# A hybrid GLA/SSD layer: output gate, second norm and weight addresses rearranged

## The chip, the cores and the metric

The kernel is one program on one core of a Trainium2 chip. Its time is the device time in microseconds of one execution. Five engines work from queues of their own: TensorE (PE, with weight loads listed apart as PEld), VectorE (DVE), ScalarE (ACT), GpSimd (POOL) and SyncE (SP, which here issues most transfers). Each takes its instructions in the order in which the program put them there.

## What is computed

One layer over 512 latent tokens of width 1024, with 256 context tokens beside them. The part around the change, cut from the reference:

```python
ada = silu(c)[:, None, :] @ w_ada + b_ada
sh1, sc1, g1, sh2, sc2, g2 = jnp.split(ada, 6, axis=-1)
parts = _split_in(modulate(rms_norm(h_lat, norm1_w), sh1, sc1) @ w_in)   # q k v r ... z xs ... gates
# GLA branch (q, k, v, r) -> o_a @ w_pa = y_a;  SSD branch (z, xs, ...) -> o_b @ w_pb = y_b
merged = sigmoid(gate_a) * y_a + sigmoid(gate_b) * y_b
h_lat = h_lat + g1 * (merged @ w_out)
h2 = modulate(rms_norm(h_lat, norm2_w), sh2, sc2)        # h * (1 + scale) + shift
h_lat = h_lat + g2 * ((silu(h2 @ w_gate) * (h2 @ w_up)) @ w_down)
return rms_norm(h_lat, final_norm_w)
```

## The kernel before

Every large product is made of three matmuls (`mm3`): each operand is kept as a rounded high part and the low rest, and high x high, high x low and low x high add up in PSUM. Weights come as blocks of 512 KB, 128 partitions by 1024 floats. `load_raw` (L176) issues the load on SP into one of three raw buffers. `split_w` rounds the block to its high part on ACT (L188) and subtracts that on DVE (L189); `load_w` allots the two results, `whi` and `wlo`, from two buffers each. A block that doesn't find a free buffer waits there.

The program is one long row of stages: adaLN and the first norm; input projections by head (GLA) and by group (SSD), each followed by its scan; back projections `pa` and `pb` (`proj_back`, 512 columns of tokens streamed against weight columns); the merge gates; the last back projection, `pb` 3; the merge; the output projection; the second norm; the feed-forward. `proj_cols` keeps the weights stationary and streams tokens (`l_` for latent, `c_` for context). `proj_rows` (L386 to L388, for v, r and z) does the reverse: it keeps `hH` or `hL` stationary and streams 256 columns of weights. A scheduler with a model of durations sets the order within each engine's queue; weight splits have high priority in it.

In the tail, `merge(j)` is called as the columns of `pb` 3 are finished: two gate tiles are loaded, DVE adds one and multiplies by each branch (L977, L978), POOL adds the two branches (L979, `tgm`), ACT rounds the result to `mH` and DVE makes `mL` (L980, L981; the tiles are called `mt`, `mL`, `mLb`). Each `w_out` block is multiplied on POOL by the gate row `g1r` before its split (L187). The output projection (L204 to L206, `ob`) takes its first four weight blocks over all four token tiles, then blocks 4 to 7 (the last two in `w67`, shown as `w`) tile by tile, so that tile 0 finishes first.

Per tile of 128 tokens, DVE then adds `ob` to `hres` (L1012), ACT squares with a sum (L1014), DVE and POOL make the reciprocal root (`hs`, `rv_h`, `rr_h`), DVE multiplies the row by it and by the scale row (L1021, `hn`) and adds the shift row (L1022; one of eight on POOL), PE transposes (L1025, `hT`), ACT and DVE split the result into `h2H` and `h2L` (L1028, L1029). The scale and shift rows are loaded from a copy of the adaLN vector in DRAM and spread over 128 partitions. The low parts of the first two gate and up blocks are made on POOL (`split_pool`). These two blocks are multiplied in halves of 256 tokens (L1057 to L1059), the later ones, from j = 2, over 512.

Pad tiles at both ends of SBUF (`top_pad`, `low_pad`) are there so that the large tiles begin at multiples of 256 bytes; all weight, `hH` and `hL` operands of the three-matmul products do. `some_ada` computes later columns of the adaLN vector on POOL, a block at a time.

Of the kernel before, what the change touches and what calls it, by code (L numbers as in the profile page):

```python
# [129 lines left out]
def hybrid_layer_kernel(ctx: ExitStack, tc: tile.TileContext, x, xc, wts, vec, rows, up, msk, lvl, out):  # L130
# [808 lines left out]
    nc.sync.dma_start(g1r.rearrange("p (j c) -> p j c", c=P), arow[0:1, 16:24, :].to_broadcast([P, 8, P]))

    def half_rows(name, j0):
        ts = []
        for c in range(2):
            t = ch.tile([P, 512], F32, tag="s2", name=f"{name}_{c}", bufs=7)
            nc.sync.dma_start(t.rearrange("p (j c) -> p j c", c=P), arow[0:1, j0 + 4 * c:j0 + 4 * c + 4, :].to_broadcast([P, 4, P]))
            ts.append(t)
        return ts
# [257 lines left out]
```

## Time and profile before

| | |
|---|---|
| median of 3 runs | 1394.48 us (1393.54 to 1395.78) |
| the profiled execution, its own time | 1392.06 us |
| its span, first to last instruction | 1390.3 us |
| PE busy | 1339.7 us, 96% |
| DVE busy | 854.5 us, 61% |
| ACT busy | 523.5 us, 38% |
| POOL busy | 328.0 us, 24% |
| HBM | 121 GB/s over the span |

A busy PE is a PE with a matmul in flight: matmuls overlap, and the time from the start of one to the start of the next is shorter than the record of one. The shares are means over stages with different limits.

### The profile page before, as it was taken

How to read it: one execution, taken by the hardware profiler on the slowest of the kernel's cores; microseconds unless marked ns; L12 is line 12 of the kernel's file. 1: busy time of each engine (PE TensorE's matmuls, PEld its weight loads, DVE VectorE, ACT ScalarE, POOL GpSimd, SP SyncE). 2: the span in 40 equal slices, each digit the busy share in tenths (PEclk: the TensorE clock that was granted, in tenths of full speed). 3: DMA queues.
4: the chain of work that ended last, by engine and by line, in shares of the span. 5: the costliest groups of instructions: out<-in, count | busy, mean ns of one | idle time of the engine just before them, and what ended most of it. 6: DMA issues, size and time to landing. Idle time of an engine off the chain costs nothing.

```text
span 1390.3 us, 19141 instructions
## 1 busy us (share of the span) xinstructions
PE 1339.7 (96%) x7462; PEld 1140.9 (82%) x7462; DVE 854.5 (61%) x1317; ACT 523.5 (38%) x924; POOL 328.0 (24%) x277
## 2 busy tenths in 40 slices
PE   5998999999999999999999999999889999999997
PEld 3797999889889788878878887777688888888886
DVE  4659686572695687668769776668673433333235
ACT  6475343433445142633524352332333223222122
POOL 1356455244100211021021102116631312100001
PEclk9899999999999999999999999999999999999999
DMA  9453322423322333223323233557413333333331
GB/s 366 141 198 121 101 101 92 128 81 132 103 81 85 126 124 106 89 87 92 114 80 116 87 121 98 189 166 252 153 60 121 123 120 122 122 106 91 94 113 67
DMA packets 58010, 169.19 MB, mean 122 GB/s; under 512 B 6064, under 2 KB 10304, under 8 KB 57792
## 3 DMA queue, kind: packets, MB, share of 16 engines
q1 hardware_dynamic: 55328, 157.96, 34.6%
q0 software_dynamic: 2304, 9.64, 2.2%
q8 instruction: 59, 0.97, 0.3%
q10 hardware_dynamic: 288, 0.36, 0.1%
q14 instruction: 31, 0.25, 0.1%
HBM read 156.23 MB, written 11.72 MB: 121 GB/s over the span
## 4 chain that ended last, share of the span: by engine, by line
PE 82%; DVE 7%; DMA 6%; issue 2%; ACT 2%; POOL 2%; SPq 0%; POOLq 0%; DVEq 0%; ACTq 0%
PE up L1059 3%; PE gate L1058 3%; PE up L1058 3%; PE gate L1059 3%; PE gate L1057 3%; PE up L1057 3%; PE db L204 3%; PE db L205 3%; PE db L206 3%; DMA E<-cdr 2%; PE yi L501 2%; PE r_z L386 2%; PE r_z L388 2%; PE r_z L387 2%; PE l_xs L361 2%; PE pb_pb L633 2%
## 5 line engine op out<-in xcount | busy, mean ns | idle before, releaser
L341 POOL TENSOR_TENSOR raw_ada<-raw_ada,cs 128x1024 f32<-128x1024 f32 x32 | 66.9, 2090 | 279.0 <-DMA raw_ada<-in_wts_dram 233.1
L343 POOL TENSOR_TENSOR raw_ada<-raw_ada 128x512 f32<-128x512 f32 x64 | 77.6, 1213 | 4.3
L386 PE MATMUL r_z<-whi_z,hH 128*128 128x256 f32 x256 | 74.0, 289 | 0.9 <-DVE cv_x L663 0.9
L388 PE MATMUL r_z<-whi_z,hL 128*128 128x256 f32 x256 | 72.9, 285 | 0.0
L387 PE MATMUL r_z<-wlo_z,hH 128*128 128x256 f32 x256 | 72.8, 285 | 0.0
L1058 PE MATMUL gate<-h2L,whi_gate 128*128 128x512 f32 (+1 forms) x192 | 71.7, 373 | 0.0
L1057 PE MATMUL gate<-h2H,whi_gate 128*128 128x512 f32 (+1 forms) x192 | 71.7, 374 | 0.0
L1059 PE MATMUL gate<-h2H,wlo_gate 128*128 128x512 f32 (+1 forms) x192 | 71.4, 372 | 0.0
L753 ACT ACTIVATE E<-E,ebias 128x128 f32<-128x128 f32 x128 | 41.2, 391 | 65.1 <-DVE E L750 65.1
L1059 PE MATMUL up<-h2H,wlo_up 128*128 128x512 f32 x160 | 63.0, 394 | 0.0
L1058 PE MATMUL up<-h2L,whi_up 128*128 128x512 f32 x160 | 62.3, 389 | 0.0
L1057 PE MATMUL up<-h2H,whi_up 128*128 128x512 f32 x160 | 62.2, 389 | 0.0
L189 DVE TENSOR_TENSOR wlo_down<-raw_down,whi_down 128x1024 fp32r<-128x1024 f32 x18 | 22.0, 1225 | 62.4 <-ACT whi_down L188 62.3
L189 DVE TENSOR_TENSOR wlo_gate<-raw_gate,whi_gate 128x1024 fp32r<-128x1024 f32 x20 | 31.1, 1557 | 45.7 <-ACT whi_gate L188 45.7
L386 PE MATMUL r_v<-whi_v,hH 128*128 128x256 f32 x192 | 55.7, 290 | 0.4 <-ACT whi_v L188 0.4
L205 PE MATMUL db<-wlo_down,fH 128*128 128x512 f32 x142 | 55.2, 389 | 0.0
L206 PE MATMUL db<-whi_down,fL 128*128 128x512 f32 x142 | 55.2, 389 | 0.0
L388 PE MATMUL r_v<-whi_v,hL 128*128 128x256 f32 x192 | 55.1, 287 | 0.0
L387 PE MATMUL r_v<-wlo_v,hH 128*128 128x256 f32 x192 | 54.6, 284 | 0.0
L632 PE MATMUL pb_pb<-yT,whi_pb 128*128 128x512 f32 x128 | 54.2, 425 | 0.0
L1066 DVE TENSOR_TENSOR f<-f,up 128x512 f32<-128x512 f32 x22 | 15.1, 687 | 63.1 <-PE up L1059 62.5
L188 ACT ACTIVATE whi_gate<-raw_gate 128x1024 fp32r<-128x1024 f32 x22 | 23.3, 1060 | 76.7 <-PE gate L1058 67.2
...
## 6 DMA issues: line engine op xcount, KB each, us to landing
...
```

Source lines behind the costliest of these rows:

```text
L189: (nc.gpsimd if split_pool[0] else nc.vector).tensor_tensor(lo, raw, hi.bitcast(F32), ALU.subtract)
L205: nc.tensor.matmul(out_, aH, bL, start=False, stop=False)
L206: nc.tensor.matmul(out_, aL, bH, start=False, stop=stop)
L341: nc.gpsimd.tensor_tensor(raw, raw, cs[:, :, 0:1].to_broadcast([P, KD, P]), ALU.mult)
L343: nc.gpsimd.tensor_tensor(raw[:, 0:n, :], raw[:, 0:n, :], raw[:, n:2 * n, :], ALU.add)
L386: nc.tensor.matmul(o, hH[:, kk, tk], hi[:, k, :], start=st, stop=False, skip_group_check=True)
L387: nc.tensor.matmul(o, hH[:, kk, tk], lo[:, k, :], start=False, stop=False, skip_group_check=True)
L388: nc.tensor.matmul(o, hL[:, kk, tk], hi[:, k, :], start=False, stop=sp, skip_group_check=True)
L632: nc.tensor.matmul(pt, hi[:, k, cl], aH[:, k, :], start=(k == 0), stop=False)
L1057: nc.tensor.matmul(pts[kj][:, tk], hi[:, k, :], h2H[:, k, tk], start=(k == 0), stop=False)
L1058: nc.tensor.matmul(pts[kj][:, tk], hi[:, k, :], h2L[:, k, tk], start=False, stop=False)
L1059: nc.tensor.matmul(pts[kj][:, tk], lo[:, k, :], h2H[:, k, tk], start=False, stop=(k == KD - 1))
```

## The change

The gate g1 moves from the weights to the result: DVE multiplies each `ob` bank by `g1r` before it is added to `hres`. The merge's addition and the four low parts that POOL made are put on DVE.

The second norm is done by columns. ACT multiplies the rows by the reciprocal root alone (`hn`); PE transposes two token tiles into four banks, in which a channel is a partition; there scale and shift are one number per partition, and ACT (`h2H`) and DVE (`hv`, then `h2L`) apply them to 256 tokens at a time. The row copies of scale, shift and norm weight, with their six transfers, are gone, and only the 16 rows of g1 go through DRAM. The last eight columns of the adaLN vector start three feed-forward blocks later.

The `whi` and `wlo` buffers become 1088 floats long. Blocks of 256 columns (v, r, z, pa, pb) begin 48 floats, 192 bytes, into them; all others at their start, a multiple of 256 bytes.

```diff
-    def split_w(key, hi, lo, row=None):
+    def split_w(key, hi, lo):
         with nullcontext() if in_start[0] else tc.high_priority():
             raw = load_raw(key)
-            if row is not None:
-                nc.gpsimd.tensor_tensor(raw[:, 0, :], raw[:, 0, :], row, ALU.mult)
             nc.scalar.activation(hi, raw, AF.Copy)
-            (nc.gpsimd if split_pool[0] else nc.vector).tensor_tensor(lo, raw, hi.bitcast(F32), ALU.subtract)
+            nc.vector.tensor_tensor(lo, raw, hi.bitcast(F32), ALU.subtract)
...
-        hi = wp.tile([P, nk, ncol], F32R, tag="whi", name="whi_" + nm)
-        lo = wp.tile([P, nk, ncol], F32R, tag="wlo", name="wlo_" + nm)
+        c0 = 48 if ncol == 256 else 0
+        hi, lo = (wp.tile([P, 1088], F32R, tag="w" + p, name=f"w{p}_{nm}")[:, c0:c0 + nk * ncol].rearrange("p (k c) -> p k c", k=nk)
+                  for p in ("hi", "lo"))
...
-    nc.tensor.transpose(pt[0:96, 0:P], ada.rearrange("p j t -> p (j t)"), ident)
+    nc.tensor.transpose(pt[0:16, 0:P], ada[:, 16:24, :].rearrange("p j t -> p (j t)"), ident)
...
-    sh2 = half_rows("sh2", 24)
-    sc2 = half_rows("sc2", 32)
...
-        nc.vector.scalar_tensor_tensor(sc2[c], sc2[c], 1.0, n2, ALU.add, ALU.mult)
+    s2c = cst.tile([P, 64], F32, name="s2c")[:, 0:KD]
+    nc.vector.scalar_tensor_tensor(s2c, ada[:, 32:40, 0], 1.0, vecs[:, V_N2:V_N2 + KD], ALU.add, ALU.mult)
...
-        nc.gpsimd.tensor_tensor(ta, ta, tb, ALU.add)
+        nc.vector.tensor_tensor(ta, ta, tb, ALU.add)
...
-            nc.vector.tensor_tensor(hres[i][:, cl], hres[i][:, cl], ob[i][c], ALU.add)
             o = ch.tile([P, 512], F32, tag="z", name=f"o_{i}_{c}", bufs=4)
+            nc.vector.tensor_tensor(o, ob[i][c], g1r[:, cl], ALU.mult)
+            nc.vector.tensor_tensor(hres[i][:, cl], hres[i][:, cl], o, ALU.add)
             nc.scalar.activation(o, hres[i][:, cl], AF.Square, accum_out=sq[:, c:c + 1])
...
+        if i % 2 == 0:
+            pts = [sm_bank(f"hT_{i}_{q}") for q in range(4)]
         for half in range(2):
             xn = ch.tile([P, 512], F32, tag="z", name=f"hn_{i}_{half}", bufs=4)
-            nc.vector.scalar_tensor_tensor(xn, hres[i][:, half * 512:(half + 1) * 512], r, sc2[half], ALU.mult, ALU.mult)
-            (nc.gpsimd if (i, half) == (2, 1) else nc.vector).tensor_tensor(xn, xn, sh2[half], ALU.add)
...
+            nc.scalar.activation(xn, hres[i][:, half * 512:(half + 1) * 512], AF.Copy, scale=r)
             for k in range(4):
-                nc.tensor.transpose(pt[:, k * P:(k + 1) * P], xn[:, k * P:(k + 1) * P], ident)
...
+                kk = half * 4 + k
+                c0 = (kk % 2) * 256 + (i % 2) * P
+                nc.tensor.transpose(pts[kk // 2][:, c0:c0 + P], xn[:, k * P:(k + 1) * P], ident)
+        if i % 2 == 1:
+            tk = slice((i - 1) * P, (i + 1) * P)
+            for k in range(KD):
+                pv = pts[k // 2][:, (k % 2) * 256:(k % 2) * 256 + 256]
+                sc, sh = s2c[:, k:k + 1], ada[:, 24 + k, 0:1]
+                nc.scalar.activation(h2H[:, k, tk], pv, AF.Identity, bias=sh, scale=sc)
+                hv = ch.tile([P, 256], F32, tag="s2", name=f"h2_{i}_{k}", bufs=7)
+                nc.vector.tensor_scalar(hv, pv, sc, sh, ALU.mult, ALU.add)
+                nc.vector.tensor_tensor(h2L[:, k, tk], hv, h2H[:, k, tk].bitcast(F32), ALU.subtract)
...
-        if j0 >= 2:
+        if j0 >= 5:
             some_ada()
```

The three places in the queues on which the prediction draws follow; the line numbers are each kernel's own, and all work ahead of the merge keeps its order. First DVE's queue where the output projection runs, before; `tgm` are the merge's tiles, `wlo_out` the low parts of `w_out`:

```order
L189 TENSOR_TENSOR wlo_out_1_8885<-raw_out_1_8886,whi_out_1_8884 128x1024
L978 SCALAR_TENSOR_TENSOR tgm_3_1_8738<-tgm_3_1_8738,acc_b_4761 128x512
L981 SCALAR_TENSOR_TENSOR mt_1_8634<-tgm_2_0_8715,mt_0_8633 128x512
L978 SCALAR_TENSOR_TENSOR tgm_4_1_8766<-tgm_4_1_8766,acc_b_4761 128x512
L189 TENSOR_TENSOR wlo_out_2_8916<-raw_out_2_8917,whi_out_2_8915 128x1024
L981 SCALAR_TENSOR_TENSOR mt_1_8634<-tgm_3_0_8737,mt_0_8633 128x512
L981 SCALAR_TENSOR_TENSOR mL_0_8635<-tgm_4_0_8765,mt_0_8633 128x512
L978 SCALAR_TENSOR_TENSOR tgm_5_1_8788<-tgm_5_1_8788,acc_b_4761 128x512
L189 TENSOR_TENSOR wlo_out_3_8947<-raw_out_3_8948,whi_out_3_8946 128x1024
L978 SCALAR_TENSOR_TENSOR tgm_6_1_8816<-tgm_6_1_8816,acc_b_4761 128x512
```

And after, over the same two weight blocks:

```order
L963 SCALAR_TENSOR_TENSOR tgm_4_1_8754<-tgm_4_1_8754,acc_b_4761 128x512
L185 TENSOR_TENSOR wlo_out_1_8872<-raw_out_1_8873,whi_out_1_8871 128x1024
L964 TENSOR_TENSOR tgm_4_0_8753<-tgm_4_0_8753,tgm_4_1_8754 128x512
L963 SCALAR_TENSOR_TENSOR tgm_5_1_8776<-tgm_5_1_8776,acc_b_4761 128x512
L964 TENSOR_TENSOR tgm_5_0_8775<-tgm_5_0_8775,tgm_5_1_8776 128x512
L966 SCALAR_TENSOR_TENSOR mL_0_8623<-tgm_4_0_8753,mt_0_8621 128x512
L966 SCALAR_TENSOR_TENSOR mL_1_8624<-tgm_5_0_8775,mt_0_8621 128x512
L185 TENSOR_TENSOR wlo_out_2_8902<-raw_out_2_8903,whi_out_2_8901 128x1024
L963 SCALAR_TENSOR_TENSOR tgm_6_1_8804<-tgm_6_1_8804,acc_b_4761 128x512
L963 SCALAR_TENSOR_TENSOR tgm_7_1_8826<-tgm_7_1_8826,acc_b_4761 128x512
L964 TENSOR_TENSOR tgm_6_0_8803<-tgm_6_0_8803,tgm_6_1_8804 128x512
L964 TENSOR_TENSOR tgm_7_0_8825<-tgm_7_0_8825,tgm_7_1_8826 128x512
```

The additions L964 stand between the merge's other passes, where POOL made them before, and the splits stand later among them.

Next ACT's queue where the second norm begins, before; `o` are the squares, with the sums `hss`:

```order
L188 ACTIVATE w_up_9233<-raw_up_0_9240 128x1024
L188 ACTIVATE whi_gate_0_9234<-raw_gate_0_9236 128x1024
L1014 ACTIVATE o_0_0_9030,hss_0_9028<-hres_0_8625 128x512
L1014 ACTIVATE o_0_1_9033,hss_0_9028<-hres_0_8625 128x512
L188 ACTIVATE w_up_9233<-raw_up_1_9250 128x1024
L1014 ACTIVATE o_1_0_9087,hss_1_9085<-hres_1_8626 128x512
L1014 ACTIVATE o_1_1_9090,hss_1_9085<-hres_1_8626 128x512
L188 ACTIVATE whi_gate_1_9244<-raw_gate_1_9246 128x1024
L1028 ACTIVATE h2H_9002<-hT_0_0_9044 128x4x128
```

And after:

```order
L184 ACTIVATE w_up_9261<-raw_up_0_9268 128x1024
L184 ACTIVATE whi_gate_0_9262<-raw_gate_0_9264 128x1024
L184 ACTIVATE w_up_9261<-raw_up_1_9278 128x1024
L1000 ACTIVATE o_0_0_9009,hss_0_9008<-hres_0_8613 128x512
L1000 ACTIVATE o_0_1_9013,hss_0_9008<-hres_0_8613 128x512
L1010 ACTIVATE hn_0_0_9027<-hres_0_8613,rr_h0_9021 128x512
L1010 ACTIVATE hn_0_1_9033<-hres_0_8613,rr_h0_9021 128x512
L1000 ACTIVATE o_1_0_9064,hss_1_9063<-hres_1_8614 128x512
L1000 ACTIVATE o_1_1_9068,hss_1_9063<-hres_1_8614 128x512
L1010 ACTIVATE hn_1_0_9078<-hres_1_8614,rr_h1_9076 128x512
L1010 ACTIVATE hn_1_1_9084<-hres_1_8614,rr_h1_9076 128x512
L184 ACTIVATE whi_gate_1_9272<-raw_gate_1_9274 128x1024
```

The second `w_up` split now stands ahead of the first squares, the products `hn` between squares of one tile and the next, and the split of the second gate block behind the `hn` of tile 1.

Last PE's queue at the end of the output projection, before; `hT_i_half` are transposes:

```order
L1025 MATMUL hT_0_0_9044<-idt_77,hn_0_0_9041 128x128 x4
L1025 MATMUL hT_0_1_9054<-idt_77,hn_0_1_9051 128x128 x4
L204 MATMUL ob_3_1_8852<-w67_8991,mt_1_8634 128x512
L205 MATMUL ob_3_1_8852<-w67_8991,mt_1_8634 128x512
L206 MATMUL ob_3_1_8852<-w67_8991,mLb_1_8638 128x512
L1025 MATMUL hT_1_0_9101<-idt_77,hn_1_0_9098 128x128 x4
L1025 MATMUL hT_1_1_9111<-idt_77,hn_1_1_9108 128x128 x4
L1057 MATMUL gate_0_9263<-h2H_9002,whi_gate_0_9234 128x256
L1057 MATMUL up_0_9264<-h2H_9002,w_up_9233 128x256
```

And after, where a bank holds two channels of two tiles:

```order
L1014 MATMUL hT_0_1_9024<-idt_77,hn_1_0_9078 128x128 x2
L1014 MATMUL hT_0_2_9025<-idt_77,hn_1_1_9084 128x128 x2
L1014 MATMUL hT_0_3_9026<-idt_77,hn_1_1_9084 128x128 x2
L1049 MATMUL gate_0_9291<-h2H_8982,whi_gate_0_9262 128x256
L1049 MATMUL up_0_9292<-h2H_8982,w_up_9261 128x256
L1050 MATMUL gate_0_9291<-h2L_8983,whi_gate_0_9262 128x256
L1051 MATMUL gate_0_9291<-h2H_8982,wlo_gate_0_9263 128x256
L1050 MATMUL up_0_9292<-h2L_8983,w_up_9261 128x256
L1051 MATMUL up_0_9292<-h2H_8982,w_up_9261 128x256
L1049 MATMUL gate_0_9291<-h2H_8982,whi_gate_0_9262 128x256
L1049 MATMUL up_0_9292<-h2H_8982,w_up_9261 128x256
L1014 MATMUL hT_2_0_9161<-idt_77,hn_2_0_9165 128x128 x2
```

The last output matmul is followed by the transposes of tile 1 in both; then gate and up begin, and after eight of them stands the first transpose of tile 2, which stood behind 46 of them before.

## Rows read from the trace of the kernel before

**Rows 1.** Busy time of each engine by stretch; columns as in the first line.
```profile
core 0: us, PE busy (x) PEld busy (x) DVE busy (x) ACT busy (x) POOL busy (x), PEclk, DMA share, GB/s
55.00:934.20 879.20, 866.88 (x5222) 752.45 (x5220) 621.93 (x1025) 366.34 (x702) 221.53 (x192) 1.00 0.35 113
...
956.40:1010.20 53.80, 46.30 (x201) 36.20 (x199) 38.98 (x37) 18.63 (x27) 35.59 (x18) 1.00 0.49 154
1010.20:1042.85 32.65, 28.05 (x218) 27.21 (x218) 23.14 (x28) 10.04 (x19) 9.81 (x8) 0.95 0.16 49
1042.85:1390.30 347.45, 339.61 (x1523) 281.84 (x1522) 127.46 (x149) 93.42 (x122) 41.35 (x35) 1.00 0.34 108
```

**Rows 2.** PE's timeline: start, us, line, tiles, count, idle before and releaser.
```profile
956.39 1.30 PE L204 MATMUL ob<-whi_out,mt 128*128 128x512 f32 x5
...
967.27 1.52 PE L204 MATMUL ob<-whi_out,mt 128*128 128x512 f32 x6
971.18 0.50 PE L205 MATMUL ob<-wlo_out,mt 128*128 128x512 f32 x1 [2.39 <-DVE wlo_out L189]
...
1008.61 1.03 PE L1025 MATMUL hT<-idt,hn 128*128 128x128 f32 x8
...
1009.95 0.40 PE L206 MATMUL ob<-w,mLb 128*128 128x512 f32 x1
1014.78 1.97 PE L1025 MATMUL hT<-idt,hn 128*128 128x128 f32 x8 [4.44 <-DVE hn L1022]
...
1017.85 0.54 PE L1058 MATMUL gate<-h2L,whi_gate 128*128 128x256 f32 x1
```

**Rows 3.** Groups by form, 930 to 1050 us: busy us, mean ns, idle before.
```profile
L187 POOL TENSOR_TENSOR raw_out<-raw_out,g1r 128x1024 f32<-128x1024 f32 x8 | 21.9, 2735 | 5.9 <-DMA raw_out<-in_wts_dram 4.9 <-ACT mt L980 0.7 <-issue 0.4
...
L979 POOL TENSOR_TENSOR tgm<-tgm,tgm 128x512 f32<-128x512 f32 x8 | 13.3, 1667 | 17.3 <-DVE tgm L978 9.6 <-DVE tgm L977 6.3 <-POOL raw_out L187 0.7
...
L1021 DVE SCALAR_TENSOR_TENSOR hn<-hres,rr_h,sc 128x512 f32<-128x512 f32 x8 | 10.9, 1398 | 2.1 <-POOL rr_h L170 2.0
L978 DVE SCALAR_TENSOR_TENSOR tgm<-tgm,acc_b 128x512 f32<-128x512 f32 x8 | 9.6, 1201 | 5.9 <-DMA tgm<-tdr 5.8
...
L981 DVE SCALAR_TENSOR_TENSOR mt<-tgm,mt 128x512 fp32r<-128x512 f32 x4 | 8.2, 2052 | 0.0
...
L1014 ACT ACTIVATE o<-hres 128x512 f32<-128x512 f32 x8 | 5.0, 623 | 1.4 <-DVE hres L1012 1.4
```

**Rows 4.** DVE's timeline around the last back projection and the output projection.
```profile
942.73 0.68 DVE L981 SCALAR_TENSOR_TENSOR mt<-tgm,mt 128x512 fp32r<-128x512 f32 x1
...
949.22 2.88 DVE L981 SCALAR_TENSOR_TENSOR mt<-tgm,mt 128x512 fp32r<-128x512 f32 x1
...
969.91 1.21 DVE L189 TENSOR_TENSOR wlo_out<-raw_out,whi_out 128x1024 fp32r<-128x1024 f32 x1
```

**Rows 5.** POOL's timeline at the same place.
```profile
948.17 3.38 POOL L187 TENSOR_TENSOR raw_out<-raw_out,g1r 128x1024 f32<-128x1024 f32 x1
```

**Rows 6.** The chain of what ended last: start, us, what.
```profile
992.40 3.48 DMA raw_up<-in_wts_dram
```

**Rows 7.** Lines L657 and L698: durations in ns, min/median/max.
```profile
L657 ACT ACTIVATE cv_x<-c_xs,vecs x16: 552/554/569, 390.4 to 812.9; 128x256 f32<-128x256 f32 x16
...
L698 DVE SCALAR_TENSOR_TENSOR z<-z,r_z x32: 404/412/422, 433.4 to 824.4; 128x256 f32<-128x256 f32 x32
```

**Rows 8.** PE's timeline in a z projection, first and 22nd in a row.
```profile
421.41 0.28 PE L388 MATMUL r_z<-whi_z,hL 128*128 128x256 f32 x1
...
423.92 0.28 PE L388 MATMUL r_z<-whi_z,hL 128*128 128x256 f32 x1
```

**Rows 9.** Tile r_z, first of its three lines: ns min/median/max.
```profile
L386 PE MATMUL r_z<-whi_z,hH x256: 278/283/469, 421.0 to 820.1; 128*128 128x256 f32 x128
```

**Rows 10.** PE's groups by form, whole span: context matmuls of 256 columns.
```profile
L368 PE MATMUL c_xs<-hH,wlo_xs 128*128 128x256 f32 x128 | 36.0, 281 | 0.0
```

**Rows 11.** The same view: a back projection and the down projection, 512 columns.
```profile
L205 PE MATMUL db<-wlo_down,fH 128*128 128x512 f32 x142 | 55.2, 389 | 0.0
...
L634 PE MATMUL pb_pb<-yT,wlo_pb 128*128 128x512 f32 x128 | 50.4, 400 | 0.0
```

More of the change, by code (lines that the diff above doesn't have):

```diff
@@ L39 @@
 V_TOT = 200
-R_GN, R_DS, R_DTB, R_AL, R_SN, R_FN, R_N2 = 0, 256, 288, 352, 416, 2464, 3488
-R_TOT = 4512
+R_GN, R_DS, R_DTB, R_AL, R_SN, R_FN = 0, 256, 288, 352, 416, 2464
+R_TOT = 3488
 M_ID, M_LE, M_GE, M_GT, M_LT, M_ONE = range(6)
@@ L198, in load_w @@
         nm = "_".join(map(str, key))
-        hi = wp.tile([P, nk, ncol], F32R, tag="whi", name="whi_" + nm)
-        lo = wp.tile([P, nk, ncol], F32R, tag="wlo", name="wlo_" + nm)
-        return split_w(key, hi, lo, row)
+        c0 = 48 if ncol == 256 else 0
+        hi, lo = (wp.tile([P, 1088], F32R, tag="w" + p, name=f"w{p}_{nm}")[:, c0:c0 + nk * ncol].rearrange("p (k c) -> p k c", k=nk)
+                  for p in ("hi", "lo"))
+        return split_w(key, hi, lo)
     def mm3(out_, aH, aL, bH, bL, start, stop):
@@ L931, in hybrid_layer_kernel @@
     pt = sm_bank("adaT")
-    nc.tensor.transpose(pt[0:96, 0:P], ada.rearrange("p j t -> p (j t)"), ident)
-    adT = ch.tile([96, P], F32, tag="s2", name="adT", bufs=7)
-    nc.vector.tensor_copy(adT, pt[0:96, 0:P])
-    adr = dr.tile([96, P], F32, name="adr")
+    nc.tensor.transpose(pt[0:16, 0:P], ada[:, 16:24, :].rearrange("p j t -> p (j t)"), ident)
+    adT = ch.tile([16, P], F32, tag="s2", name="adT", bufs=7)
+    nc.vector.tensor_copy(adT, pt[0:16, 0:P])
+    adr = dr.tile([16, P], F32, name="adr")
     nc.gpsimd.dma_start(adr, adT)
-    arow = adr.rearrange("(j t) p -> t j p", t=2)
     g1r = pj.tile([P, D], F32, tag="p4", name="g1r")
[L939 to L947, printed above, removed]
-    sh2 = half_rows("sh2", 24)
-    sc2 = half_rows("sc2", 32)
-    for c in range(2):
-        n2 = ch.tile([P, 512], F32, tag="s2", name=f"n2_{c}", bufs=7)
-        nc.sync.dma_start(n2, rows[0:1, R_N2 + c * 512:R_N2 + (c + 1) * 512].to_broadcast([P, 512]))
-        nc.vector.scalar_tensor_tensor(sc2[c], sc2[c], 1.0, n2, ALU.add, ALU.mult)
+    nc.sync.dma_start(g1r.rearrange("p (j c) -> p j c", c=P),
+                      adr.rearrange("(j t) p -> t j p", t=2)[0:1].to_broadcast([P, 8, P]))
+    s2c = cst.tile([P, 64], F32, name="s2c")[:, 0:KD]
+    nc.vector.scalar_tensor_tensor(s2c, ada[:, 32:40, 0], 1.0, vecs[:, V_N2:V_N2 + KD], ALU.add, ALU.mult)
     hp.close()
@@ L993, in hybrid_layer_kernel @@
     for k in range(4):
-        hi, lo = load_w(("out", k), g1r)
+        hi, lo = load_w(("out", k))
         for i in range(4):
@@ L997, in hybrid_layer_kernel @@
                 rows_mm(ob, mH, mL, k, i, hi[:, 0], lo[:, 0], c, 7)
-    ow = [load_w(("out", k), g1r) for k in (4, 5)]
+    ow = [load_w(("out", k)) for k in (4, 5)]
     w67 = ch.tile([P, 4, 1024], F32R, tag="h16", name="w67")
     for n, k in enumerate((6, 7)):
-        ow.append(split_w(("out", k), w67[:, 2 * n:2 * n + 1, :], w67[:, 2 * n + 1:2 * n + 2, :], g1r))
+        ow.append(split_w(("out", k), w67[:, 2 * n:2 * n + 1, :], w67[:, 2 * n + 1:2 * n + 2, :]))
     h2H = f2.tile([P, KD, SEQ], F32R, tag="hH", name="h2H")
@@ L1177, in lay_out @@
         a["gla_norm_w"][0], a["d_skip"][0], a["dt_bias_f"][0], a["dt_bias_b"][0], a["a_log_f"][0], a["a_log_b"][0],
-        a["ssm_norm_w"][0], a["final_norm_w"], a["norm2_w"][0]]).reshape(1, R_TOT)
+        a["ssm_norm_w"][0], a["final_norm_w"]]).reshape(1, R_TOT)
     up = np.zeros((96, 2, 512), f32)
```

10 lines of the change are left out of this document (1 added, 9 removed).

## Prediction

> **What bounds the kernel now.** I cut the span at the seams of the program and read TensorE (PE) against each stretch first [rows 1]. From 55 to 934.2 us PE is busy for 866.88 of 879.20 us, in the feed-forward after 1042.85 for 339.61 of 347.45. There only the number of matmuls or the time from one to the next can matter. Between the last back projection and the feed-forward it is otherwise: in the output projection, 956.40 to 1010.20, PE is busy for 46.30 of 53.80 us, and in the second norm with the first two gate/up blocks, to 1042.85, with 28.05 of 32.65 and a mean granted clock of 0.95.
>
> Next I read PE in those two stretches [rows 2]. Its 192 output matmuls could follow each other every 0.2267 us: the first at 956.39, the 49th at 967.27, so 48 in 10.88. That is 43.5 us, and with the transposes that stand among them (eight, from 1008.61, 0.1 us each) 44.3, so the last could end at 1000.7; it starts at 1009.95. The row 971.18 says what PE waited for: the low half of a weight block, from VectorE (DVE). After the last one PE idles for 4.44 us for the normalised rows (`hn`), again from DVE, and the gate matmuls are continuous only from 1017.85.
>
> Why is DVE late? Grouped by form in this part [rows 3], GpSimd (POOL) multiplies each output weight block by the gate row, 2.735 us each, and merges the branches, 1.667 us each. DVE's 512-column passes L1021, L978 and L981 have means of 1.40, 1.20 and 2.05 us. One and the same operation, L981, takes 0.68 us at 942.73 and 2.88 at 949.22 [rows 4]; most of the second lies inside POOL's 3.38 us from 948.17 [rows 5]. So the 20 passes of the three groups cost 28.7 us instead of 20 x 0.68 = 13.6: some 15 us of DVE time are POOL's presence.
>
> **The change, part by part.**
>
> *POOL out of the tail.* The eight gate multiplies (21.9 us) and eight merges (13.3) leave POOL, and four weight splits and one addition with them. What remains there are the four `rr`. I let DVE run at its undisturbed durations and take the splits of `w_out` by what is left in front of them: a block lands, ScalarE (ACT) rounds it, DVE subtracts. POOL's 2.7 us fall out of that line.
>
> *What DVE gets.* Added: eight gate multiplies on the output and eight merges, 16 x 0.68; four splits at 1.21 [rows 4]; sixteen `hv` and sixteen 256-column subtractions, 32 x 0.41 (by the 256-column DVE row with a PSUM source [rows 7]): 28.8 us. Removed: eight L1021, seven L1022, eight old `h2L`, two L955, 25 x 0.68 = 17.0. Net +11.8, against the 15 of stretching that go, so DVE has about as much to do as before, but in another place: more of it stands behind the output projection.
>
> *Output projection.* Walking the new queue orders with these durations: blocks 0 to 4 no longer hold PE up; before block 5 some 0.5 us stay, because its place in the line of raw buffers comes free only when an earlier split has read the block in it. So its end moves from 1010.2 to 1000.7 + 0.5 = 1001.2: **-9.0 us**.
>
> *Second norm.* ACT takes `hn` (0.62 each by L1014 [rows 3]) and sixteen biased passes of 0.554 [rows 7]. New waits stand in both queues. ACT now has the second `w_up` split ahead of the first squares: its block takes the buffer of the first, issued near 990 and landing near 994, by the 3.48 us of such a block [rows 6]. DVE has the low half of it between the first two tiles' additions, and the second gate block's between the third tile's. Behind them stand the squares, `hn` and PE's transposes of tile 0, and after those the last six output matmuls. Working along: squares of tile 0 done 997.9, `hn` 1000, tile 1's squares 1001.2, `rr` 1002.3, `hn` 1003.6, transposes 1004.5, ACT's gate split and first `h2H` 1006, first `h2L` 1007. Gate/up runs continuously from about 1007.9. Then one column block feeds 4 x 3 matmuls of 0.12 us, 1.44 us, while DVE makes one in 0.8 us, so DVE keeps ahead unless the additions of tiles 2 and 3, which stand between, hold it. PE also meets the first transpose of tile 2 after only eight gate/up matmuls and waits for it until about 1008.7. With 192 x 0.12 = 23 us, the transposes of tiles 2 and 3 (sixteen, 1.6) and 0.9 us for such stops, the block ends near 1033.4 instead of 1042.85: **-9.4 us together with the term above**. I take -9. Bounds: -14 if PE has no stop at all (1000.7, 3 us of norm, 23.0 and 1.6 make 1028.3), -4 if DVE's half of the first two tiles comes 5 us later.
>
> *Smaller parts.* The six row broadcasts of norm 2 and their place on SP's queue go; PE starts the output projection directly behind the back projection already (956.39), so nothing is gained there. The 16-row transpose in place of 96 is one instruction: 0. The late ada loads start three blocks later in the feed-forward, where PE is busy 98%: 0.
>
> *The 192 bytes.* The v, r and z blocks stream 256 columns of weights against stationary activations; their start moves from a multiple of 256 bytes to 192 beyond one, while the stationary tiles stay. There are 768 + 576 + 384 = 1,728 such matmuls. From 421.41 to 423.92 are 21 of their steps [rows 8], 0.120 us each; 256 columns at 2.4 GHz are 106.7, so 13 ns of each are something else. No row of before has this operand at 192. Nearest rows: the shortest r_z record is 278 ns against a median of 283 [rows 9], so single steps 5 ns shorter exist at the old address; context matmuls of the same width, which stand between others of 512 columns, average 281 [rows 10]. I take those 281, the nearer row, -2 ns: 1,728 x -2 = **-3.5 us**. Bounds: the 5 ns of the shortest record, -8.6, and in mirror +8.6; all 13 ns gone, -22.5, or doubled, +22.5. The back projections' stationary blocks get the same start: 576 matmuls of 512 columns; their L634 averages 400 ns where the same form of the down projection has 389 [rows 11]. I take 0, since stops are in that mean; the 11 ns could go or come again, -6.3 to +6.3.
>
> The Trainium skill ("TensorE: Matmul & The Clock Gate", Step-by-step: what each phase is for) says that the streamed operand and the weight load have read ports of their own, so that a load doesn't take bandwidth from a running matmul. By that rule an address could not matter and the term would be 0; that the 13 ns exist says that the rule leaves something out, but not that the address is it. The same page (Wait — 56ns, not 53.3ns?) gives N / 2.4 GHz + 2.5 ns for bf16; by it, an estimate, the step would be 109 and the term -18; the shortest r_z row is 5 ns under the median, not 10.
>
> **Sum.** 1392.06 (profiled) - 9 - 3.5 = 1379.6; the median of the runs, 1394.48, stands 2.4 higher, so **1382.0**.
>
> **The rivals.**
>
> A, as above: 1376 to 1388. Chance 0.42.
>
> B, the address is the cause of most of the 13 ns. For it: something regular adds them to each 256-column and each 512-column step alike (226.7 against 213.3), and the load of the next weights runs beside every matmul. Against: the context matmuls, where weight block and activations have changed roles, have nearly the same step [rows 10], as if it came with any matmul. With -7 to -13 ns: 1394.5 - 9 - 12.1 = 1373.4, down to 1363; middle 1368. Chance 0.18.
>
> C, the address does nothing: 1394.5 - 9 = 1385.5. For it speaks the same steadiness of the step, whatever the tile. By the two-port rule of the Trainium skill ("TensorE: Matmul & The Clock Gate") this would be the answer. Chance 0.17.
>
> D, DVE and ACT become the bound in the tail. They get the `w_up` and gate splits in front of the norm, +11.8 us of passes at undisturbed speed, and the merge additions in the line to `mH`. If the split of block 7 or the additions run 5 us behind, PE idles for what it idled for before, then the tail gives 0 to -4; with the address term or without it that is 1387 to 1394.5, middle 1391. For it: PE's stops of before were DVE's already. Against: the 15 us of stretching. Chance 0.13.
>
> E, slower: the new start lengthens the step. Weight load and stream would now meet where before they passed; the price is 1.73 us for each ns. From +5.2 ns on, the tail's gain is used up, from +6.8 ns the kernel is slower by over 0.2%; doubling the 13 ns gives 1394.5 - 9 + 22.5 = 1408. For it: the pair of addresses is in no row of before, so nothing excludes it. Against: rows vary by less. Chance 0.10.
>
> **How the numbers follow.** What a measurement can tell from no change is about 0.2%, 2.8 us: faster is below 1391.7, slower above 1397.3. Faster: A, B, C and more than half of D, 0.85. Same: the rest of D and E between +3.6 and +6.8 ns, 0.09. Slower: the rest of E, 0.06. The range from 1367 to 1391 leaves out the lower part of B (0.07), the top of D (0.04) and E (0.08).
>
> **What would show it.** In the profile after: no POOL operation longer than 1 us from 943 to 1033; DVE's 512-column passes at 0.68; the last output matmul near 1001; the first feed-forward block of one (j = 2) near 1033; 256-column r_z records with a median of 281 (A), 270 to 276 (B), 283 (C), over 290 (E), with l_ and db unchanged at 389. Wrong would be a gate/up stretch with PE waiting for `h2L` or `hn` by more than 3 us (D), or any lengthening of stretches ahead of 934 but v, r and z.

## The result, and the profile after

The changed kernel takes 1382.53 us (median of 4 runs, 1378.9 to 1385.32), the kernel before beside it 1394.01 (1390.96 to 1395.78). The ratio is 0.9917 with a 95% interval of 0.9901 to 0.9933: 11.5 us faster, at 1382.0 predicted. The profiled execution took 1385.32, the longest of the four, with a span of 1383.5; the profiled one of before was among the shorter of its kind. So the two traces differ by 6.7 us, less than the medians, and below each stretch is compared by itself. In this pair the tail, from the first output matmul to block j = 2, is 8.4 us shorter and the feed-forward from there 0.2, while everything ahead of the tail takes 1.8 us longer, the shorter steps of v, r and z notwithstanding; the experiments come back to this.

The windows of the profile after, over the same stretches as [rows 1]; the seams lie 1.8 us later here, and 6.6 us earlier from the last on:

```profile
core 0: us, PE busy (x) PEld busy (x) DVE busy (x) ACT busy (x) POOL busy (x), PEclk, DMA share, GB/s
55.00:934.20 879.20, 861.67 (x5215) 746.22 (x5214) 626.22 (x1026) 365.75 (x700) 218.24 (x192) 1.00 0.35 112
...
956.40:1010.20 53.80, 49.89 (x228) 40.57 (x226) 34.31 (x51) 23.98 (x39) 1.65 (x3) 0.99 0.47 151
1010.20:1042.85 32.65, 32.65 (x230) 31.50 (x229) 18.60 (x40) 15.48 (x27) 0.54 (x1) 0.92 0.15 49
```

PE (TensorE) is now busy all through the second of the two tail stretches, and POOL (GpSimd) has left both: 1.65 and 0.54 us against 35.59 and 9.81. The clock granted in the last stretch is lower than before, 0.92 against 0.95. That window has its first 26 us from the norm's gate/up and the rest from block j = 2. PE's timeline after, the places of [rows 2] and the first matmul of the feed-forward block j = 2:

```profile
958.20 1.31 PE L202 MATMUL ob<-whi_out,mt 128*128 128x512 f32 x5
...
1000.37 1.03 PE L1014 MATMUL hT<-idt,hn 128*128 128x128 f32 x8
...
1002.40 0.40 PE L204 MATMUL ob<-w,mLb 128*128 128x512 f32 x1
1003.32 1.27 PE L1014 MATMUL hT<-idt,hn 128*128 128x128 f32 x8 [0.52 <-ACT hn L1010]
1005.34 0.39 PE L1049 MATMUL gate<-h2H,whi_gate 128*128 128x256 f32 x1 [0.74 <-ACT h2H L1020]
...
1007.66 0.39 PE L1050 MATMUL gate<-h2L,whi_gate 128*128 128x256 f32 x1 [1.82 <-DVE h2L L1023]
...
1009.74 0.69 PE L1014 MATMUL hT<-idt,hn 128*128 128x128 f32 x2 [0.83 <-ACT hn L1010]
...
1036.12 0.40 PE L1049 MATMUL gate<-h2H,whi_gate 128*128 128x512 f32 x1
```

And that matmul before:

```profile
1042.68 0.40 PE L1057 MATMUL gate<-h2H,whi_gate 128*128 128x512 f32 x1
```

From the first to the last start of an output matmul are 44.2 us (53.6 before), with no stop. From there to the first matmul of j = 2 are 33.7 (32.7 before). Of the four short stops that are left three name ScalarE (ACT) and the longest VectorE (DVE). The stretch from 1007.66, in which gate/up runs with but one stop, by itself:

```profile
1007.66:1036.12 28.46, 27.63 (x206) 27.21 (x207) 18.49 (x41) 14.22 (x26) 1.08 (x2) 0.88 0.10 35
```

The groups by form, 930 to 1050 us, that answer to [rows 3]:

```profile
L1022 DVE TENSOR_SCALAR h<-hT,s2c,ada 128x256 f32<-128x256 f32 x16 | 8.1, 538 | 3.7 <-ACT h2H L1020 3.5
...
L963 DVE SCALAR_TENSOR_TENSOR tgm<-tgm,acc_b 128x512 f32<-128x512 f32 x8 | 5.5, 690 | 1.8 <-DMA tgm<-tdr 1.6
...
L1010 ACT ACTIVATE hn<-hres,rr_h 128x512 f32<-128x512 f32 x8 | 5.3, 716 | 3.7 <-POOL rr_h L170 3.7
...
L998 DVE TENSOR_TENSOR o<-ob,g1r 128x512 f32<-128x512 f32 x8 | 5.2, 681 | 0.0
...
L966 DVE SCALAR_TENSOR_TENSOR mt<-tgm,mt 128x512 fp32r<-128x512 f32 x4 | 2.7, 683 | 0.0
```

L963 and L966 are the L978 and L981 of before: 690 and 683 ns against 1201 and 2052. The two forms that are new to the kernel take longer than I put them, `hv` (L1022, shown as `h`) 538 ns for 410 and `hn` (L1010) 716 for 623. The groups of r_z and r_r:

```profile
L384 PE MATMUL r_z<-whi_z,hH 128*128 128x256 f32 x256 | 73.2, 286 | 0.7 <-DVE cv_x L661 0.6
L386 PE MATMUL r_z<-whi_z,hL 128*128 128x256 f32 x256 | 72.1, 282 | 0.0
L385 PE MATMUL r_z<-wlo_z,hH 128*128 128x256 f32 x256 | 72.1, 282 | 0.0
...
L384 PE MATMUL r_r<-whi_r,hH 128*128 128x256 f32 x128 | 37.2, 291 | 0.0
...
L386 PE MATMUL r_r<-whi_r,hL 128*128 128x256 f32 x128 | 36.3, 283 | 0.0
L385 PE MATMUL r_r<-wlo_r,hH 128*128 128x256 f32 x128 | 36.0, 281 | 0.0
```

Before, the first of each three:

```profile
L386 PE MATMUL r_z<-whi_z,hH 128*128 128x256 f32 x256 | 74.0, 289 | 0.9 <-DVE cv_x L663 0.9
...
L386 PE MATMUL r_r<-whi_r,hH 128*128 128x256 f32 x128 | 37.7, 295 | 0.0
```

The nine groups (three each of r_z, r_v, r_r) add up to 490.4 us against 496.1 before: 5.7 us for 1,728 matmuls, 3.3 ns each. The six of pa and pb add up to 235.2 against 234.6. The sign that the prediction named, the first line of tile r_z (ns, min/median/max; [rows 9] before):

```profile
L384 PE MATMUL r_z<-whi_z,hH x256: 276/281/468, 424.4 to 821.7; 128*128 128x256 f32 x128
```

### The profile page after: what moved, and what is told of

Same layout as the page of the kernel before. It is cut to its first block, busy times and chain, and to the rows that moved or that the text cites. A ratio compares the mean times of both kernels' runs of the same rounds, so it can differ in the third digit from the quotient of the medians.

```text
span 1383.5 us, 19137 instructions
## 1 busy us (share of the span) xinstructions
PE 1336.6 (97%) x7462; PEld 1138.6 (82%) x7462; DVE 849.2 (61%) x1345; ACT 531.8 (38%) x940; POOL 279.0 (20%) x256
## 4 chain that ended last, share of the span: by engine, by line
PE 82%; DMA 6%; DVE 6%; ACT 3%; POOL 1%; issue 1%; SPq 0%; POOLq 0%; ACTq 0%; DVEq 0%
PE up L1051 3%; PE gate L1051 3%; PE gate L1049 3%; PE up L1050 3%; PE gate L1050 3%; PE up L1049 3%; PE db L202 3%; PE db L204 3%; PE db L203 3%; PE pb_pb L631 2%; PE pb_pb L632 2%; PE pb_pb L630 2%; PE yi L499 2%; PE l_xs L359 2%; PE r_z L384 2%; PE l_xs L364 2%
## 5 line engine op out<-in xcount | busy, mean ns | idle before, releaser
L339 POOL TENSOR_TENSOR raw_ada<-raw_ada,cs 128x1024 f32<-128x1024 f32 x32 | 63.3, 1978 | 313.0 <-DMA raw_ada<-in_wts_dram 278.0
L341 POOL TENSOR_TENSOR raw_ada<-raw_ada 128x512 f32<-128x512 f32 x64 | 80.7, 1260 | 4.4
L185 DVE TENSOR_TENSOR wlo_gate<-raw_gate,whi_gate 128x1024 fp32r<-128x1024 f32 x22 | 36.9, 1679 | 46.6 <-ACT whi_gate L184 46.6
L359 PE MATMUL l_xs<-hH,whi_xs 128*128 128x512 f32 x128 | 51.9, 405 | 0.0
```

What stands on the lines that cost most here:

```text
L339: nc.gpsimd.tensor_tensor(raw, raw, cs[:, :, 0:1].to_broadcast([P, KD, P]), ALU.mult)
L341: nc.gpsimd.tensor_tensor(raw[:, 0:n, :], raw[:, 0:n, :], raw[:, n:2 * n, :], ALU.add)
L359: nc.tensor.matmul(lat, hi[:, k, :], hH[:, k, 0:SEQ], start=st, stop=False)
```

## The experiments

All are compared with the kernel before on the same chip; the rows come from several chips, so the ratios, not the medians, are what can be set side by side. "Output" is the time from the first to the last start of an output matmul on PE, "norm" from there to the start of block j = 2, both of the profiled execution. Before: 53.6 and 32.7. One execution is not the next: in the six with the changed kernel's tail as it is (changed, e1, e3, e10, e7, e8) the output part is 44.2 each time, but the norm is 32.6 to 33.9.

| kernel | median us | ratio, 95% interval | output | norm |
|---|---|---|---|---|
| changed | 1382.53 | 0.9917 (0.9901 to 0.9933) | 44.2 | 33.7 |
| e1, no shift | 1384.87 | 0.9930 (0.9916 to 0.9944) | 44.2 | 33.9 |
| e2, shift alone | 1392.86 | 0.9983 (0.9974 to 0.9992) | 53.4 | 33.1 |
| e3, shift of v, r, z only | 1379.82 | 0.9896 (0.9881 to 0.9912) | 44.2 | 32.6 |
| e4, gate alone | 1398.75 | 1.0033 (1.0018 to 1.0048) | 46.6 | 45.3 |
| e9, gate, POOL's work on DVE, norm by rows | 1391.43 | 0.9970 (0.9959 to 0.9981) | 44.4 | 39.2 |
| e11, norm by columns without the gate | 1396.13 | 1.0004 (0.9993 to 1.0015) | 55.7 | 32.7 |
| e5, splits back on POOL | 1383.39 | 0.9917 (0.9900 to 0.9933) | 44.5 | 32.9 |
| e6, merges back on POOL | 1380.55 | 0.9896 (0.9883 to 0.9909) | 44.2 | 31.2 |
| e12, both on POOL, shift of v, r, z only | 1383.60 | 0.9902 (0.9881 to 0.9922) | 44.2 | 33.2 |
| e10, shift of pa, pb only | 1386.30 | 0.9940 (0.9928 to 0.9952) | 44.2 | 33.5 |
| e7, 64 bytes, v, r, z only | 1379.95 | 0.9897 (0.9869 to 0.9924) | 44.2 | 33.1 |
| e8, 128 bytes, v, r, z only | 1383.80 | 0.9914 (0.9894 to 0.9934) | 44.2 | 32.9 |

The theory was the prediction's sum: the tail by some 9 us, and the shorter step of v, r and z by what the trace after shows. The rivals: the whole of it is one of the two; or a shorter step only moves PE's waits.

### Address and tail apart: e1, e2, e3

e1 takes the shift out of the changed kernel:

```diff
-        c0 = 48 if ncol == 256 else 0
+        c0 = 0
```

> The changed kernel with the v, r, z, pa and pb blocks back at multiples of 256 bytes; nothing else differs. Theory: the step of the v, r and z matmuls goes back from about 116 to 120 ns and that of pa and pb from 229 to 228, so the time rises by 1728 x 3.5 ns - 576 x 1 ns = 5.5 us over the changed kernel, to about 1388. Rival, the shorter steps are given back where TensorE then waits longer for its neighbours: the time stays within 1.5 us of the changed kernel. Rival, the whole gain is the address: the time goes back to the kernel before, 1394.

e2 puts it alone into the kernel before:

```diff
-        hi = wp.tile([P, nk, ncol], F32R, tag="whi", name="whi_" + nm)
-        lo = wp.tile([P, nk, ncol], F32R, tag="wlo", name="wlo_" + nm)
+        c0 = 48 if ncol == 256 else 0
+        hi, lo = (wp.tile([P, 1088], F32R, tag="w" + p, name=f"w{p}_{nm}")[:, c0:c0 + nk * ncol].rearrange("p (k c) -> p k c", k=nk)
+                  for p in ("hi", "lo"))
```

> The kernel before with the one edit that v, r, z, pa and pb blocks begin 192 bytes into longer buffers. Theory: 5.5 us faster than the kernel before, 1388.5, with the tail from 956 to 1043 as long as before, 86.5 us. Rival, given back in waits: 1393 to 1395.

e3 keeps it for three of the five kinds of block:

```diff
-        c0 = 48 if ncol == 256 else 0
+        c0 = 48 if key[0] in ("v", "r", "z") else 0
```

> The changed kernel with 192 bytes for v, r and z alone; pa and pb blocks at a multiple of 256. Theory: the 512-column steps of pa and pb, in which the shifted block is the stationary operand, fall back from 229.1 to 228.1 ns on average and the time by 0.6 us, less than the runs can tell; the 256-column steps stay at 116. Rival, the shift of pa and pb costs more than its own steps (waits behind it): over 1.5 us faster than the changed kernel.

Both parts are there. The tail alone (e1) brings 9.8 us by its ratio, the address alone (e2) 2.4, and both intervals exclude no change. But neither time is the one expected: e1 lies some 2 us over the changed kernel, between the theory's 5.5 and the rival's 1.5, and e2's 1392.86 is close to the rival's 1393 to 1395. Tile r_r shows the step in all three, first of its lines, ns min/median/max; e1:

```profile
L384 PE MATMUL r_r<-whi_r,hH x128: 277/283/469, 89.8 to 346.1; 128*128 128x256 f32 x128
```

e2:

```profile
L387 PE MATMUL r_r<-whi_r,hH x128: 276/276/469, 88.5 to 343.6; 128*128 128x256 f32 x128
```

283 with the blocks at 0, 276 at 192, whatever the tail. e1 has the longer buffers too, so it is the start in them and not their length that does it. But the time follows the steps only in part. e2's steps are some 5 us shorter in sum and its runs 2.4; e3 and e1, which differ in the shift of v, r and z alone and ran side by side, lie 5.0 apart. Part of the answer stands in PE's waits from 55 to 934.2 us: what waited for what, us, times, longest. After:

```profile
PE gc L499 <- DMA g<-gdr: 4.5, 2, 3.2
```

e3:

```profile
PE gc L499 <- DMA g<-gdr: 3.8, 1, 3.8
```

e1:

```profile
PE gc L499 <- DMA g<-gdr: 2.0, 1, 2.0
```

`g` goes to DRAM and back; where PE gets to it sooner, it may only wait for it longer. In the seven profiles with 64 or 192 bytes on v, r and z this wait is 2.7 to 4.5 us, in the seven without (e8's 128 bytes counted with these) 0 to 3.3. The ranges overlap. So do the starts of the output projection, ahead of which all fourteen run the same matmuls: 954.3 to 961.0 us in the seven, 956.4 to 959.2 in the others. How much of the steps arrives, 2.4 or 5 us, stays open, and one pair of profiles can't tell it. The shift of pa and pb adds 0.6 us in steps; that it costs the 2.7 us by which e3 lies under the changed kernel (its rival asked for over 1.5) isn't settled, as their intervals overlap and e10 (below) lies 1.4 over e1.

### The tail taken apart: e4, e9, e11

e4 is the kernel before with the gate moved:

```diff
-            if row is not None:
-                nc.gpsimd.tensor_tensor(raw[:, 0, :], raw[:, 0, :], row, ALU.mult)
...
-            nc.vector.tensor_tensor(hres[i][:, cl], hres[i][:, cl], ob[i][c], ALU.add)
             o = ch.tile([P, 512], F32, tag="z", name=f"o_{i}_{c}", bufs=4)
+            nc.vector.tensor_tensor(o, ob[i][c], g1r[:, cl], ALU.mult)
+            nc.vector.tensor_tensor(hres[i][:, cl], hres[i][:, cl], o, ALU.add)
```

> The kernel before with the gate moved from the rows of w_out to the output; merge additions and four weight splits stay on GpSimd, the second norm by rows, addresses as before. Theory (GpSimd's presence stretches VectorE and stands in the line of the weight blocks): half of the tail's gain, the output projection shorter by 4 to 6 us, the norm longer by 1 to 2 us for eight more passes: 1390 to 1392. Rival, the merge additions alone keep VectorE and the output projection as late as before: 1394 or above.

It is slower than before, 1.0033, where the theory had a gain; the rival's time is met, but not for its reason, since the output part is 7 us shorter. What of stops is left there, 2.4 us, waits for ScalarE. The norm grew by 12.6, not by 1 or 2. Its PE timeline, the first stops after the output projection:

```profile
1006.58 1.26 PE L1024 MATMUL hT<-idt,hn 128*128 128x128 f32 x8 [2.45 <-DVE hn L1021]
1016.49 1.12 PE L1024 MATMUL hT<-idt,hn 128*128 128x128 f32 x4 [8.65 <-DVE hn L1021]
...
1022.20 0.58 PE L1057 MATMUL gate<-h2L,whi_gate 128*128 128x256 f32 x1 [1.87 <-DVE h2L L1028]
```

PE idles 8.65 us, to 1016.49, for the `hn` of the second tile. DVE's timeline there:

```profile
1010.14 1.79 DVE L1016 TENSOR_TENSOR hs<-hss 128x1 f32<-128x1 f32 x1 [1.80 <-ACT o L1013]
...
1012.03 1.28 DVE L1028 TENSOR_TENSOR h2L<-hT,h2H 128x512 fp32r<-128x512 f32 x2
1013.23 1.40 DVE L1020 SCALAR_TENSOR_TENSOR hn<-hres,rr_h,sc 128x512 f32<-128x512 f32 x2
1014.55 1.28 DVE L1011 TENSOR_TENSOR o<-ob,g1r 128x512 f32<-128x512 f32 x2
1015.75 2.99 DVE L1021 TENSOR_TENSOR hn<-hn,sh 128x512 f32<-128x512 f32 x2
1018.66 2.88 DVE L1012 TENSOR_TENSOR hres<-hres,o 128x512 f32<-128x512 f32 x2
```

POOL's at the same place:

```profile
1009.57 2.34 POOL L187 TENSOR_TENSOR wlo_gate<-raw_gate,whi_gate 128x1024 fp32r<-128x1024 f32 x1 [6.29 <-ACT whi_gate L186]
...
1015.72 2.47 POOL L339 TENSOR_TENSOR raw_ada<-raw_ada,cs 128x1024 f32<-128x1024 f32 x1 [2.97 <-DMA raw_ada<-in_wts_dram]
1018.27 2.73 POOL L341 TENSOR_TENSOR raw_ada<-raw_ada 128x512 f32<-128x512 f32 x2
```

In the stop stand the gate's new passes for the next tile (`o`, 1.28 us), the low parts of the first (`h2L`), and a sum of one number per partition (`hs`) that takes 1.79 us beside POOL's weight split. Only when the stop ends does POOL turn to a late adaLN block: the pairs of `hn` and `hres` beside it take 2.99 and 2.88 us where the pair of `o` takes 1.28. So that block, which the change moves out of this stretch and which I had put at 0, lengthens what follows by some 3 us, but it did not make the stop. The clock stays at the lower of its two levels for some 9 us more, 6 of them with PE busy (the columns are those above):

```profile
1016.50:1026.00 9.50, 6.44 (x29) 5.75 (x30) 9.14 (x12) 2.53 (x6) 6.70 (x6) 0.52 0.18 55
```

e9 adds to e4 the rest of what leaves POOL, and keeps the norm by rows:

```diff
-        nc.gpsimd.tensor_tensor(ta, ta, tb, ALU.add)
+        nc.vector.tensor_tensor(ta, ta, tb, ALU.add)
...
-    split_pool[0] = True
...
-            (nc.gpsimd if (i, half) == (2, 1) else nc.vector).tensor_tensor(xn, xn, sh2[half], ALU.add)
+            nc.vector.tensor_tensor(xn, xn, sh2[half], ALU.add)
```

> The kernel before with the gate on the output and all merge additions, splits and norm additions on VectorE, the second norm still by rows, addresses as before: the changed kernel's tail without the norm by columns. Theory: the output projection ends as early as in the changed kernel (10 us sooner), but the norm's VectorE chain per tile (o, hres, hn, shift, h2L: some 6 us a tile, with nothing on ScalarE to share it) makes TensorE wait between the halves; tail gain 2 to 5 us of the 8.4, 1390 to 1392. Rival (the norm's form does not matter, only GpSimd's presence did): 1386.

As the theory has it: the output part is that of the changed kernel, the norm 5.5 us longer than there. PE's stop ahead of the second tile's transposes is 5.73 us, for the last of DVE's passes per row:

```profile
1009.81 1.11 PE L1024 MATMUL hT<-idt,hn 128*128 128x128 f32 x4 [5.73 <-DVE hn L1021]
...
1021.73 1.23 PE L1024 MATMUL hT<-idt,hn 128*128 128x128 f32 x8 [1.09 <-DVE hn L1021]
```

The adaLN block is in e9 too, and comes after that stop, in POOL's timeline:

```profile
1011.67 3.44 POOL L339 TENSOR_TENSOR raw_ada<-raw_ada,cs 128x1024 f32<-128x1024 f32 x1 [5.70 <-DVE h2L L1028]
```

There it holds up the third tile's reciprocal root, which POOL makes behind it; VectorE waits 3.05 us for that, and PE 1.09 at 1021.73.

e11 is the other half, the norm by columns with the gate left on POOL and on the weights:

```diff
-            nc.vector.tensor_tensor(o, ob[i][c], g1r[:, cl], ALU.mult)
-            nc.vector.tensor_tensor(hres[i][:, cl], hres[i][:, cl], o, ALU.add)
+            nc.vector.tensor_tensor(hres[i][:, cl], hres[i][:, cl], ob[i][c], ALU.add)
```

(shown against the changed kernel; the multiply of the weight rows, POOL's merges and splits and the starts at multiples of 256 are put back with it).

> The norm by columns alone: gate on the rows of w_out by GpSimd, merges and splits on GpSimd, all blocks at multiples of 256, as in the kernel before; beside it only the later start of the last adaLN columns. Theory (the gate multiplies keep the output projection late, the norm's form only shortens what follows): output projection as long as before within 1 us, the stretch from its end to the block j = 2 shorter by 2 to 5 us, 1390 to 1393. Rival (the norm by columns brings the whole of the tail's gain): 1386.

No change, 1.0004. The output part is 2 us longer than before and still has its stops, in PE's timeline:

```profile
975.19 0.50 PE L207 MATMUL ob<-wlo_out,mt 128*128 128x512 f32 x1 [1.77 <-DVE wlo_out L189]
...
983.05 0.50 PE L207 MATMUL ob<-wlo_out,mt 128*128 128x512 f32 x1 [1.47 <-DVE wlo_out L189]
...
990.07 0.50 PE L207 MATMUL ob<-wlo_out,mt 128*128 128x512 f32 x1 [1.29 <-DVE wlo_out L189]
```

and the norm is as long as before, not 2 to 5 us shorter: theory and rival both miss. So neither part gains alone; e12 (below), which has both and keeps POOL's merges and splits, has the whole gain. The gate's move frees the output projection and pays it back in the norm; the norm by columns gains nothing by itself and keeps the norm at 33 us when eight more DVE passes stand in it. The later start of the adaLN columns is in e11 and e12 and not in e4 and e9, and was not tried alone: how much of the norm's 39 and 45 us it would take away is open, but the longest stop in each stood before the block began or was all but over.

### What POOL may keep: e5, e6, e12

e5 gives the four splits back to POOL, e6 the eight additions, e12 both (with e3's shift):

```diff
-            nc.vector.tensor_tensor(lo, raw, hi.bitcast(F32), ALU.subtract)
+            (nc.gpsimd if split_pool[0] else nc.vector).tensor_tensor(lo, raw, hi.bitcast(F32), ALU.subtract)
```

```diff
-        nc.vector.tensor_tensor(ta, ta, tb, ALU.add)
+        nc.gpsimd.tensor_tensor(ta, ta, tb, ALU.add)
```

> The changed kernel with the low parts of the first two gate and up blocks made by GpSimd again, as in the kernel before; all else as changed. Theory (GpSimd's long two-source passes stretch VectorE in the norm): the four passes of 2.4 us lie on 990 to 1006, VectorE's additions, hv and h2L beside them go from 0.68 to over 1.2 us, and the first two blocks end 2 to 4 us later: 1385 to 1387. Rival (VectorE's queue is the bound, so every pass taken off it helps): 1 to 2 us faster than the changed kernel.

> The changed kernel with the eight merge additions on GpSimd again. Theory: each addition lies between two VectorE passes of the same column block and in the line to mH; with no gate multiply on GpSimd before it, it takes 1.3 us instead of 1.67, and TensorE's stops in the output projection come back by 1 to 3 us: 1384 to 1386. Rival (without the gate multiplies GpSimd is idle enough, the additions are off the line): same as the changed kernel within 1 us.

> The changed kernel with GpSimd keeping its merge additions and its four weight splits, and the 192 bytes for v, r and z alone: of the change the gate on the output, the norm by columns and the shift of v, r, z are left. Theory after the runs before this (only GpSimd's gate multiplies were in the way; what it does else is off VectorE's queue for nothing): tail 9 to 11 us shorter than before, steps 5 us, 1378 to 1380, the fastest of all. Rival (GpSimd's presence costs when both kinds are kept together): 1383 or above.

The theory falls in e5 and e6: neither costs anything that these runs can tell, the output part is 44.2 to 44.5 us in all three. e5's rival, 1 to 2 us faster, isn't seen either. e6's norm is the shortest, 31.2. Its windows show less of the lower clock:

```profile
1000.00:1010.20 10.20, 7.18 (x43) 6.32 (x42) 9.46 (x22) 7.42 (x18) 1.10 (x2) 0.83 0.19 53
1010.20:1045.00 34.80, 34.80 (x236) 32.28 (x235) 17.58 (x31) 14.94 (x22) 0.00 (x0) 1.00 0.20 63
```

That is 3.5 us at the lower level (0.83 of 10.2), and none after 1010.2; the changed kernel's stretch from 1007.66 alone has 6.8 (0.88 of 28.46). Whether the additions on POOL have to do with that, or it is one execution's luck, isn't shown. e12's tail is as short as the changed kernel's; its time is not the fastest of all, as the theory had it, though the intervals overlap. What had held PE up in the output projection was POOL's gate multiply in the line of the weight blocks, not POOL's presence as such: in e12 VectorE's splits of `w_out` beside POOL's merges still average 1424 ns, for 1222 in the changed kernel, and PE has no stop. First e12, then the changed kernel:

```profile
L187 DVE TENSOR_TENSOR wlo_out<-raw_out,whi_out 128x1024 fp32r<-128x1024 f32 x6 | 8.5, 1424 | 0.7 <-ACT whi_out L186 0.7
```

```profile
L185 DVE TENSOR_TENSOR wlo_out<-raw_out,whi_out 128x1024 fp32r<-128x1024 f32 x6 | 7.3, 1222 | 0.7 <-ACT whi_out L184 0.5 <-DMA tgm<-tdr 0.3
```

### Which distance: e10, e7, e8

e10 shifts pa and pb alone, e7 and e8 v, r and z by 16 and by 32 floats in place of 48:

```diff
-        c0 = 48 if ncol == 256 else 0
+        c0 = 48 if key[0] in ("pa", "pb") else 0
```

```diff
-        c0 = 48 if ncol == 256 else 0
+        c0 = 16 if key[0] in ("v", "r", "z") else 0
```

> The changed kernel with the 192 bytes for pa and pb alone; v, r and z at a multiple of 256. Theory: their 576 steps rise by 1 ns on average, 0.6 us, so the time is that of the changed kernel without any shift, 0 to 1 us more. Rival (the shift costs pa and pb more than their own steps): 2 us or more above the changed kernel without any shift.

> The changed kernel with v, r and z 64 bytes instead of 192 beyond a multiple of 256, pa and pb not shifted. What is looked at is the step of the 256-column matmuls: by the theory that any distance from the stationary tile's start will do, 116 ns as with 192, 1380 to 1382; by the rival that 192 is special (64 bytes behind the next multiple), 119.7 as with 0, 1385.

> As the run with 64 bytes, but 128. Any distance will do: 116 ns, 1380 to 1382. Only an odd multiple of 64: 119.7 ns, 1385. Only 192: 119.7 ns.

e10 lies 1.4 us over e1, nearer the theory than the rival and within the noise of both. Tile r_r in e7, first of its lines, ns min/median/max:

```profile
L384 PE MATMUL r_r<-whi_r,hH x128: 276/279/469, 88.9 to 343.8; 128*128 128x256 f32 x128
```

The same in e8:

```profile
L384 PE MATMUL r_r<-whi_r,hH x128: 279/282/471, 88.8 to 345.4; 128*128 128x256 f32 x128
```

Medians of 283, 279, 282 and 276 ns at 0, 64, 128 and 192 bytes. A median is a poor measure here, since the records at 192 bytes lie in two clumps, near 276 and near 281, and the median of r_z there falls on the other side, at 281. The sums are better: the nine groups of v, r and z add up to 496.1, 489.1, 494.4 and 489.5 us (the last from e3): 64 and 192 bring some 7 us of steps, 128 less than 2. Of the forms expected, an odd multiple of 64 fits best, though 128 isn't quite 0. For v, r and z only the start of the streamed block moves in these runs, with the stationary tile at a multiple of 256 bytes; whether it is the distance of the two or the streamed operand's own start that counts wasn't tried.

## Why the prediction was right

**Output projection**, -9.0 predicted: -9.4. Half of the reading held: POOL's multiply ahead of each split was what PE waited for, while VectorE's stretching beside POOL's merges, the other half, costs nothing without it (e6, e12). The walk along the queues ended it 44.8 us after its first matmul; the last now starts 44.2 after the first. The 0.5 us stop before block 5 didn't come.

**Second norm**, -0.4 predicted: +1.0. Continuous gate/up came 2 us sooner than I had walked it: at 1007.66, which is 1005.9 on the time line of before, for 1007.9. `hv` and `hn` were longer than the rows that I took for them, and did not keep it from that. The rest was undersized: from there to j = 2 are 28.5 us where I had 25.5. The granted clock says what for. A mean of 0.88 over this stretch is 6.8 us at the lower of two levels, one of them in a stop; in the rest the 256-column steps are 0.21 us in place of the 0.12 with which I had counted all 192, some 2.5 of the 3.0 us. The stretch before had a mean of 0.95, so this term was there to be seen, and I put it at nothing. By the six executions with this tail the norm's change is -0.1 to +1.2. So -9 for the tail stands against -8.4. That both halves of this term need each other I had not seen: the prediction counts the gate on the output as a gain and the norm as nearly neutral, which is true only of the pair.

**POOL out of the tail** was given too much: the merges and splits could stay (e5, e6, e12). And the late adaLN block, which I put at 0, does stretch VectorE in the norm (e4), by some 3 us.

**The 192 bytes**, -3.5 predicted: -5.7 in steps for v, r and z, and +0.6 for pa and pb where I had 0. The r_z median came out at the 281 that I had named, r_r's at 276. This was luck more than reasoning: the row I chose (context matmuls, 281) begins at the old address, so nothing in it spoke for the new one, and the size was a guess. The shorter steps reach the time in part only; net 2.4 to 5, so the term was right in what it brought, by two errors that cancel.

One sign that I had set for being wrong did appear: the stretches ahead of the tail are 1.8 us longer in the trace after. As the output projection starts at 954.3 in e5 and at 958.2 in the changed kernel, with the same code ahead of it, that says little.

The port rule that I weighed for this term, of the Trainium skill ("TensorE: Matmul & The Clock Gate", Step-by-step: what each phase is for), has nothing on start addresses, and I drew from it that the step would stay; it changed with nothing but the start address, so here the measurement decides against that conclusion. The other rule of the Trainium skill, N / 2.4 GHz + 2.5 ns (the same page, Wait — 56ns, not 53.3ns?), makes an estimate of 109 ns for the step; no run's mean gets there, the lowest is some 115.5 (e2).

**The rivals.** B and C are out (the steps changed, by 3.3 ns and not by 7 or 0), E too. D has something for it in another kernel than the changed one: with the gate on the output and the norm by rows (e4, e9), PE's longest stop in the norm waits for VectorE, and e4 is slower than before.
